# One conformer block on one core: the first FFN's SiLU products turned by the DMA crossbar instead of TensorE, and its adaLN rows read on another schedule

## The chip, the cores and the metric

The kernel runs on one core of a Trainium2 chip. The metric is the device time of one execution in microseconds (us). Before the change three executions gave a median of 1824.64 us (1823.7 to 1827.11).

## What is computed

One block of a macaron network on 256 tokens of width 2048, in float32: FFN, mixer (differential attention beside a causal depthwise convolution), FFN. Nine modulation vectors come from one product of `silu(c)` with `w_ada` (adaLN), three for each part: shift, scale and gate.

```python
ada = silu(c) @ w_ada + b_ada
sh1, sc1, g1, shm, scm, gm, sh2, sc2, g2 = split(ada, 9)
h = modulate(rms_norm(x, ffn1_norm), sh1, sc1)
x = x + 0.5 * g1 * swiglu(h, ffn1_w_gu, ffn1_w_down)     # D_FF = 5632
h = modulate(rms_norm(x, mix_norm), shm, scm)
x = x + gm * hybrid_mixer(h, ...)
h = modulate(rms_norm(x, ffn2_norm), sh2, sc2)
x = x + 0.5 * g2 * swiglu(h, ffn2_w_gu, ffn2_w_down)

def swiglu(h, w_gu, w_down):
    g, u = split(h @ w_gu, 2)
    return (silu(g) * u) @ w_down
```

## The kernel before, in words

**Weight tiles.** Every weight matrix is read in tiles of 1 MB, `raw` (128 partitions x 4 x 512 float32), by DMAs that SyncE issues in order (SP's queue, line 295; four `raw` buffers). To multiply float32 in the faster fp32r format, each half of a tile is split in two: ScalarE rounds it to `whi` (line 306), VectorE subtracts to get the rest, `wlo` (line 308); there are four `whi` and four `wlo` buffers of half a tile. TensorE then makes three products for each of the 4 x 2 pairs of a 128-row slice and a token half (lines 330, 334, 335), 24 matmuls of 512 columns a tile.

**The first half of an FFN.** The 5632 columns of gate and up are cut into 22 chunks of 256 + 256 columns, each with four weight tiles (2048 rows in fours of 512). The first pass of the rows for all chunks comes first (`stage_a`, while the norm and the modulation are still being made), then in the first FFN some later rows of the chunks 3 to 14 (the lists `EARLY`). What is left is done chunk by chunk in the loop over `groups`: chunks 0 to 2 together, then each alone. In the first FFN chunks 3 to 12 have two tiles left there, 13 and 14 one, 15 to 21 three. In the second FFN chunks 3 to 5 have two left, all later ones three.

**`finish(c)`**, the code under change, runs one weight tile after a chunk's last product. VectorE adds the partial sums out of PSUM (line 854, once for each token half), ScalarE takes SiLU (line 855), VectorE multiplies by up (line 856). The down product needs the result with the columns on the partitions, so it must be turned. That is `rest()`, put off by one more weight tile (`after_tiles(1, rest)`). In the first FFN TensorE turns it, with four 128 x 128 transposes into PSUM (line 875). In the second FFN the DMA crossbar does: ScalarE first copies the float32 words into two planes of 16-bit halves (line 860, `planes`), a DMA transpose on SP's queue turns both (line 866, `turned`), and ScalarE puts the halves together again (line 869, `src`). Either way the turned product is then split like a weight, ScalarE at line 351 and VectorE at line 352.

**The adaLN rows.** `w_ada` is read in 144 rows of 1 MB into the same four `raw` buffers by the same queue (line 193); VectorE multiplies each by `silu(c)` and sums it (line 194). Where the rows stand in the program is set by two schedules. During the first part of the first FFN `DUE` gives, for so many 512-row quarters of weight tiles done, how many rows must have been asked for, with straight lines between its points. In the loop over single chunks and in the down product, `ada_share(r, limit)` asks for `r` rows a weight tile until row `limit`.

**What sets the order.** The instructions of each engine and of SP's queue are put in an order when the program is built, by a scheduler that goes by the order of the code and an estimate of when inputs are ready. On the chip each engine runs its list in that order: what waits holds up all behind it.

Of the kernel before, what the change touches and what calls it, by code (L numbers as in the profile page):

```python
# [31 lines left out]
NCH = 22  # L32
# [13 lines left out]
AGAIN = [4, 5, 6]  # L46
EARLY = [[3, 8, 9], [4, 5, 6], [7, 10, 11], [12, 13, 14]]
EARLY_3 = [13, 14]

DUE = ((8, 4), (16, 6), (22, 8), (57, 16), (108, 24), (151, 32))  # L50


TAPS = (6, 5, 6, 6, 6, 6, 8, 6, 6, 6)
# [3 lines left out]

SEVEN = (3, 5, 8, 10, 13, 15, 17)
KEPT = 6
CROSSBAR = {0: False, 96: True}  # L60
RMS_EPS = 1e-6
LN_EPS = 1e-5
LAM_INIT = 0.8 - 0.6 * float(np.exp(-0.3 * 0))
# [20 lines left out]
def block_kernel(ctx: ExitStack, tc: tile.TileContext, x_in, pos_in, w_ada, small, w_gu1, w_dn1,  # L84
# [20 lines left out]
    def blk(shape, dtype=F32):  # L105
        return blkp.tile(shape, dtype, tag="blk", name=nm("blk"))

    def tmp(shape, dtype=F32):
        return tmpp.tile(shape, dtype, tag="tmp", name=nm("tmp"))

    def sm(shape, tag="sm"):
        return smp.tile(shape, F32, tag=tag, name=nm(tag))
# [4 lines left out]
    def tp_tile(shape=(P, 512)):  # L117
        return tpp.tile(list(shape), F32, tag="tp", name=nm("tp"))
# [53 lines left out]
    def after_tiles(n, fn):  # L172
        later.append([n, fn])
# [34 lines left out]
    def ada_due(rows):  # L208

        r0, j0 = DUE[0]  # L210
        for r, j in DUE[1:]:
            if rows <= r:
# [137 lines left out]
    def split_from_psum(tp, hi, lo):  # L350
        nc.scalar.copy(out=hi, in_=tp)  # L351
        nc.vector.tensor_sub(out=lo, in0=tp, in1=hi.bitcast(F32))  # L352
# [310 lines left out]
    def ffn(st, w_gu, w_dn, gate_base, ada_a, ada_b, nxt, again, early, early_3):  # L663
# [6 lines left out]
        base = st.base  # L670
# [180 lines left out]
        def finish(c, accs):  # L851
            p = parts[c]
            for t in range(NT):
                nc.vector.tensor_add(out=p[:, t, :], in0=accs[t], in1=p[:, t, :])  # L854
                nc.scalar.activation(out=p[:, t, :256], in_=p[:, t, :256], func=AF.Silu)  # L855
                nc.vector.tensor_mul(out=p[:, t, 256:], in0=p[:, t, :256], in1=p[:, t, 256:])  # L856

            if CROSSBAR[base]:
                planes = tmp([P, 2, NT, 256], U16)
                nc.scalar.copy(out=planes, in_=p[:, :, 256:].bitcast(U16).rearrange("p t (f b) -> p b t f", b=2))  # L860

            def rest():
                a = blk([P, 2, 2, S], F32R)
                if CROSSBAR[base]:
                    turned = tmp([P, 2, NT, 2, P], U16)
                    nc.sync.dma_start_transpose(out=turned.rearrange("p b t i s -> p (b t i) s"),
                                                in_=planes.rearrange("p b t f -> p (b t f)"))
                    src = tmp([P, 2, NT, P])
                    nc.scalar.copy(out=src.bitcast(U16).rearrange("p i t (s b) -> p b t i s", b=2), in_=turned)  # L869
                    src = src.rearrange("p i t s -> p i (t s)")  # L870
                else:
                    src = tp_tile((P, 2, S))
                    for t in range(NT):
                        for i in range(2):
                            nc.tensor.transpose(src[:, i, t * P:(t + 1) * P],  # L875
                                                p[:, t, 256 + i * P:256 + (i + 1) * P], ident)
                split_from_psum(src, a[:, 0], a[:, 1])
                aT[c] = a

            after_tiles(1, rest)  # L880
# [3 lines left out]
        for g in groups:  # L884
            accs = {c: [acc_tile() for _ in range(NT)] for c in g}
            for i, (pc, ks) in enumerate(segments(g[0], start_of[g[0]], 4)):
                ada_until(base + 8 * pc + 8)
                pieces(last_part[0])
                for c in g:
                    w = w_tile(w_gu[c, pc], False, ks)  # L890
                    mm_tile(accs[c], w, act, 4 * pc, i == 0, pc == 3, (0, 1), ks)
                    ext[c] = 4
                    if len(g) > 1:
                        ada_a_share(ks[1] - ks[0])
                        pieces(last_part[0])
                    else:
                        ada_share(ada_b[0], ada_b[1])
                    if i == 0:
                        while pend:
                            finish(*pend.pop(0))  # L900
            for c in g:
                pend.append((c, accs[c]))
# [24 lines left out]
        if nxt is None:  # L927
            down_strassen(w_dn, aT, a_act, lambda: gate(gate_base, 0.5), evac_last, lambda: ada_share(*ada_b),
                          pend, finish)
            return  # L930

        prev = None
        for n in range(4):
            accs = [acc_tile() for _ in range(NT)]
            held = []
            for pc in range(11):
                hold = n == 3 and pc >= 11 - HOLD_DN
                w = w_tile(w_dn[n, pc], hold and pc > 11 - HOLD_DN)
                ada_share(ada_b[0], ada_b[1])
                if hold:  # L940
                    held.append((pc, w))
                    continue
                mm_tile(accs, w, a_act, 4 * pc, pc == 0, pc == 10)
                if pc == 0:
                    while pend:
                        finish(*pend.pop(0))
                    if prev is not None:
                        evac(*prev)
                        prev = None
                if n == 0 and pc == 6 and nxt is norm_m:  # L950
                    attention_constants()
                if n == 0 and pc == 2:
                    gbc = gate(gate_base, 0.5)
# [74 lines left out]
    norm1 = Norm(0, "n1", sm([P, NT, 4], "ss"))  # L1028
    norm_m = Norm(48, "nm", sm([P, NT, 4], "ss"), DVE_COLS)
    norm2 = Norm(96, "n2", sm([P, NT, 4], "ss"))  # L1030


    ffn(norm1, w_gu1, w_dn1, 32, (0.78, 32), (0.78, 104), norm_m, AGAIN, EARLY, EARLY_3)


    st = norm_m
# [462 lines left out]
```

## Time and profile before

| | |
|---|---|
| median of three executions | 1824.64 us |
| the profiled execution | 1823.93 us, of which the profile's span is 1822.2 us |
| TensorE (PE) busy | 1797.5 us, 99% |
| VectorE (DVE), ScalarE (ACT) busy | 1518.2 us (83%), 1023.9 us (56%) |
| read from HBM | 492.37 MB, 271 GB/s over the span |
| line 875, the first FFN's transposes | 88, between 284.0 and 528.4 us |
| line 866, the second FFN's DMA transposes | 22, between 1293.8 and 1589.6 us |

The profile is that of one execution. A row of its timeline gives start, duration, engine (SPq is SP's queue of DMA issues), line, operation and "output<-inputs" by the program's names; rows of one kind that follow each other are merged with a count. In square brackets stands the idle time before the row and what ended it. A row of the groups of lines gives busy time, mean duration in ns, and idle time ahead of it with its releasers. A row of the windows gives, for a stretch of the span, the busy time of each engine with the number of instructions, the granted TensorE clock (1.00 is full), the share in which the 16 DMA engines moved something, and what they moved in GB/s.

### The profile page before, as it was taken

How to read it: one execution, taken by the hardware profiler on the slowest of the kernel's cores; microseconds unless marked ns; L12 is line 12 of the kernel's file. 1: busy time of each engine (PE TensorE's matmuls, PEld its weight loads, DVE VectorE, ACT ScalarE, POOL GpSimd, SP SyncE). 2: the span in 40 equal slices, each digit the busy share in tenths (PEclk: the TensorE clock that was granted, in tenths of full speed). 3: DMA queues.
4: the chain of work that ended last, by engine and by line, in shares of the span. 5: the costliest groups of instructions: out<-in, count | busy, mean ns of one | idle time of the engine just before them, and what ended most of it. 6: DMA issues, size and time to landing. Idle time of an engine off the chain costs nothing.

```text
span 1822.2 us, 21874 instructions
## 1 busy us (share of the span) xinstructions
PE 1797.5 (99%) x8093; PEld 1481.0 (81%) x8093; DVE 1518.2 (83%) x2018; ACT 1023.9 (56%) x1533; POOL 28.3 (2%) x29
## 2 busy tenths in 40 slices
PE   7999999999999999999999999999999999999998
PEld 5788888888888887888888888888888888878887
DVE  7889869999888787898999798777788765599877
ACT  7554444444444343566798657675666566555453
POOL 0000000000000000000110100000000000000000
PEclk8999999999999999999999999999999999999999
DMA  9977978888889988775444487889888976655552
GB/s 378 359 304 299 351 271 300 328 322 338 338 326 352 353 342 333 292 265 208 166 158 160 152 343 255 329 326 318 265 304 303 303 244 213 206 204 216 200 217 107
DMA packets 102298, 503.26 MB, mean 276 GB/s; under 512 B 37760, under 2 KB 38192, under 8 KB 44720
## 3 DMA queue, kind: packets, MB, share of 16 engines
q1 hardware_dynamic: 102192, 501.87, 75.1%
q8 instruction: 63, 1.03, 0.2%
q14 instruction: 43, 0.35, 0.0%
HBM read 492.37 MB, written 2.12 MB: 271 GB/s over the span
## 4 chain that ended last, share of the span: by engine, by line
PE 86%; DVE 7%; ACT 3%; DMA 2%; issue 2%; POOL 0%; SPq 0%; POOLq 0%; DVEq 0%; ACTq 0%
PE acc L334 27%; PE acc L335 27%; PE acc L330 27%; DVE wlo L308 2%; DMA tmp<-tmp 1%; PE tp L334 1%; PE tp L335 1%; PE tp L330 1%; ACT whi L306 1%; DVE raw L194 1%; DMA blk<-in_w_gu_dram 1%; PE acc L1161 1%; DVE wlo L537 1%; DVE blk L1053 1%; PE tp L875 1%
## 5 line engine op out<-in xcount | busy, mean ns | idle before, releaser
L334 PE MATMUL acc<-wlo,blk 128*128 128x512 f32 x2340 | 912.7, 390 | 6.7 <-DVE wlo L308 6.6
L330 PE MATMUL acc<-whi,blk 128*128 128x512 f32 x2343 | 912.8, 392 | 1.8 <-ACT blk L404 1.3
L335 PE MATMUL acc<-whi,blk 128*128 128x512 f32 x2340 | 912.2, 390 | 0.1
L306 ACT CAST whi<-raw 128x1024 fp32r<-128x1024 f32 (+1 forms) x581 | 599.6, 1044 | 497.1 <-PE acc L335 362.8
L308 DVE TENSOR_TENSOR wlo<-raw,whi 128x1024 fp32r<-128x1024 f32 (+1 forms) x581 | 692.8, 1210 | 179.2 <-ACT whi L306 177.7
L334 PEld LDWEIGHTS acc<-wlo,blk 128*128 128x128 f32 x2340 | 439.5, 188 | 101.2 <-DVE wlo L308 11.3
L330 PEld LDWEIGHTS acc<-whi,blk 128*128 128x128 f32 x2343 | 440.0, 188 | 93.3 <-ACT blk L404 1.7
L335 PEld LDWEIGHTS acc<-whi,blk 128*128 128x128 f32 x2340 | 439.3, 188 | 92.3 <-DVE blk L406 0.7
L194 DVE CUSTOM_DVE_ANT_0 raw<-raw,c_bc 128x2048 f32<-128x2048 f32 x142 | 324.3, 2285 | 14.2 <-DMA raw<-in_w_ada_dram 14.0
L536 ACT CAST whi<-raw 128x1024 fp32r<-128x1024 f32 (+1 forms) x56 | 53.0, 946 | 67.9 <-PE tp L335 33.6
L537 DVE TENSOR_TENSOR wlo<-raw,whi 128x1024 fp32r<-128x1024 f32 (+1 forms) x56 | 60.8, 1087 | 18.9 <-ACT whi L536 18.6
L1053 DVE SCALAR_TENSOR_TENSOR blk<-blk,cst,blk 128x245 f32<-128x245 f32 (+21 forms) x176 | 70.4, 455 | 0.5 <-ACT blk L1051 0.5
L690 ACT COPY blk<-acc 128x512 f32<-128x512 f32 x72 | 41.6, 588 | 42.7 <-PE acc L335 40.1
L854 DVE TENSOR_TENSOR blk<-acc,blk 128x512 f32<-128x512 f32 x88 | 56.8, 683 | 0.2
L869 ACT COPY tmp<-tmp 128x1024 uint16<-128x1024 uint16 x22 | 29.8, 1355 | 47.4 <-DMA tmp<-tmp 47.4
L855 ACT ACTIVATE blk<-blk 128x256 f32<-128x256 f32 x88 | 34.2, 414 | 23.4 <-DVE blk L854 23.3
L330 PE MATMUL acc<-blk,blk 128*128 128x512 f32 x104 | 40.7, 395 | 0.7 <-ACT blk L322 0.7
L334 PE MATMUL acc<-blk,blk 128*128 128x512 f32 x100 | 39.1, 391 | 0.0
L335 PE MATMUL acc<-blk,blk 128*128 128x512 f32 x100 | 38.9, 393 | 0.0
L352 DVE TENSOR_TENSOR blk<-tmp,blk 128x512 fp32r<-128x512 f32 x22 | 15.1, 688 | 26.3 <-ACT blk L351 26.3
L856 DVE TENSOR_TENSOR blk<-blk 128x256 f32<-128x256 f32 x88 | 34.0, 418 | 0.2 <-ACT blk L855 0.2
L860 ACT COPY tmp<-blk 128x1024 uint16<-128x1024 uint16 x22 | 22.9, 1042 | 11.8 <-DVE blk L856 11.6
(231 smaller groups left out, 1064.2 us busy)
## 6 DMA issues: line engine op xcount, KB each, us to landing
raw<-in_w_gu_dram SPq DMA_DIRECT2D x161, 1024.0 KB, 5.9
raw<-in_w_ada_dram SPq DMA_DIRECT2D x142, 1024.0 KB, 6.3
raw<-in_w_dn_dram SPq DMA_DIRECT2D x88, 1024.0 KB, 5.1
raw<-in_w_in_dram SPq DMA_DIRECT2D x40, 1024.0 KB, 4.8
raw<-in_w_out_dram SPq DMA_DIRECT2D x16, 1024.0 KB, 5.0
raw<-in_w_gu_dram SPq DMA_DIRECT2D x8, 768.0 KB, 6.1
blk<-in_w_gu_dram SPq DMA_DIRECT2D x10, 512.0 KB, 13.8
blk<-gate_line SPq DMA_DIRECT2D x6, 512.0 KB, 5.0
```

What stands on the lines that cost most here:

```text
L194: nc.vector.tensor_tensor_reduce(out=raw, in0=raw, in1=c_bc, scale=1.0, scalar=0.0, op0=ALU.mult, op1=ALU.add, accum_out=ada_cols[g][:, j ...
L306: nc.scalar.copy(out=hi[:, :m, :], in_=rw)
L308: nc.vector.tensor_sub(out=lo[:, :m, :], in0=rw, in1=hi[:, :m, :].bitcast(F32))
L330: nc.tensor.matmul(acc, ah, wh, start=start, stop=False)
L334: nc.tensor.matmul(acc, ah, wl, start=False, stop=False)
L335: return nc.tensor.matmul(acc, al, wh, start=False, stop=stop)
L536: nc.scalar.copy(out=hi[:, :n, :], in_=src)
L537: nc.vector.tensor_sub(out=lo[:, :n, :], in0=src, in1=hi[:, :n, :].bitcast(F32))
L690: last_part[0] = nc.scalar.copy(out=parts[c][:, t, :], in_=accs[t])
L854: nc.vector.tensor_add(out=p[:, t, :], in0=accs[t], in1=p[:, t, :])
L855: nc.scalar.activation(out=p[:, t, :256], in_=p[:, t, :256], func=AF.Silu)
L1053: nc.vector.scalar_tensor_tensor(out=y[:, d:], in0=u, scalar=w, in1=y[:, d:], op0=ALU.mult, op1=ALU.add)
```

## The change

Three constants and a test. `CROSSBAR` becomes, for each FFN, the chunks whose products the crossbar turns: all 22 in both. `DUE` gets one more point, so that six more adaLN rows (32 to 37) are asked for by quarter 180 of the first part. In the first FFN's chunk loop and down product 0.7 rows come with a weight tile, not 0.78.

```diff
-DUE = ((8, 4), (16, 6), (22, 8), (57, 16), (108, 24), (151, 32))
+DUE = ((8, 4), (16, 6), (22, 8), (57, 16), (108, 24), (151, 32), (180, 38))
-CROSSBAR = {0: False, 96: True}
+CROSSBAR = {0: range(NCH), 96: range(NCH)}
...
-            if CROSSBAR[base]:
+            if c in CROSSBAR[base]:
                 planes = tmp([P, 2, NT, 256], U16)
...
             def rest():
                 a = blk([P, 2, 2, S], F32R)
-                if CROSSBAR[base]:
+                if c in CROSSBAR[base]:
                     turned = tmp([P, 2, NT, 2, P], U16)
...
-    ffn(norm1, w_gu1, w_dn1, 32, (0.78, 32), (0.78, 104), norm_m, AGAIN, EARLY, EARLY_3)
+    ffn(norm1, w_gu1, w_dn1, 32, (0.78, 32), (0.7, 104), norm_m, AGAIN, EARLY, EARLY_3)
```

VectorE's list where one of the two-tile chunks of the first FFN is finished (its partial sums and product lie in the buffer blk_254; the next chunk's are in blk_276), before:

```order
L352 TENSOR_TENSOR blk_2477<-tp_2478,blk_2477 128x512
L856 TENSOR_TENSOR blk_254<-blk_254 128x256 x2
L198 TENSOR_TENSOR ada_2306<-ada_2306,cst 128x2
L194 ISA raw_2616,ada_2306<-raw_2616,c_bc 128x2048
L194 ISA ada_2306 128x1
L308 TENSOR_TENSOR wlo_2586<-raw_2582,whi_2584 128x1024
L308 TENSOR_TENSOR wlo_2590<-raw_2582,whi_2588 128x1024
L308 TENSOR_TENSOR wlo_2629<-raw_2625,whi_2627 128x1024
```

And now:

```order
L856 TENSOR_TENSOR blk_254<-blk_254 128x256 x2
L308 TENSOR_TENSOR wlo_2564<-raw_2560,whi_2562 128x1024
L308 TENSOR_TENSOR wlo_2568<-raw_2560,whi_2566 128x1024
L194 ISA raw_2601,ada_2459<-raw_2601,c_bc 128x2048
L194 ISA ada_2459 128x1
L308 TENSOR_TENSOR wlo_2610<-raw_2606,whi_2608 128x1024
L854 TENSOR_TENSOR blk_276<-acc_2516,blk_276 128x512
L308 TENSOR_TENSOR wlo_2614<-raw_2606,whi_2612 128x1024
L352 TENSOR_TENSOR blk_2594<-tmp_2597,blk_2594 128x512
L194 ISA raw_2640,ada_2459<-raw_2640,c_bc 128x2048
L194 ISA ada_2459 128x1
L856 TENSOR_TENSOR blk_276<-blk_276 128x256
```

In both lists line 352 of a chunk stands ahead of line 856 of the next chunk. Before, its input came from TensorE's transposes (tp_2478); now it comes (tmp_2597) by way of line 860, the DMA and line 869, and four halves of weight tiles stand between line 856 and it. ScalarE's list changes with it: after the SiLU of blk_254 come two halves of a weight tile, the copy of line 860, one half, the copy of line 869, which reads what the DMA transpose wrote, one half, and line 351; all that stands behind line 869 waits for the DMA with it.

SP's queue at the same chunk; a load of w_ada is an adaLN row. Before, loads only:

```order
L193 DMA raw_2525<-in_w_ada_dram 128x2048
L295 DMA raw_2534<-in_w_gu_dram 128x2048
L193 DMA raw_2576<-in_w_ada_dram 128x2048
L295 DMA raw_2582<-in_w_gu_dram 128x2048
L193 DMA raw_2616<-in_w_ada_dram 128x2048
L295 DMA raw_2625<-in_w_gu_dram 128x2048
```

And now:

```order
L866 DMA_TRANSPOSE tmp_2506<-tmp_2469 128x8x128
L295 DMA raw_2560<-in_w_gu_dram 128x2048
L193 DMA raw_2601<-in_w_ada_dram 128x2048
L295 DMA raw_2606<-in_w_gu_dram 128x2048
L866 DMA_TRANSPOSE tmp_2595<-tmp_2558 128x8x128
L193 DMA raw_2640<-in_w_ada_dram 128x2048
L295 DMA raw_2652<-in_w_gu_dram 128x2048
```

Between two loads there is now a DMA transpose, which waits for the planes of line 860 (tmp_2558), and the loads behind it wait with it.

SP's queue ahead of the chunk loop, where the six rows go (the tiles of w_gu are the last that the lists EARLY ask for and the first of chunks 0 to 2). Before:

```order
L295 DMA raw_1928<-in_w_gu_dram 128x2048
L295 DMA raw_1990<-in_w_gu_dram 128x2048
L295 DMA raw_2024<-in_w_gu_dram 128x2048
L295 DMA raw_2058<-in_w_gu_dram 128x2048
L295 DMA raw_2092<-in_w_gu_dram 128x2048
L295 DMA raw_2126<-in_w_gu_dram 128x2048
L295 DMA raw_2160<-in_w_gu_dram 128x2048
L295 DMA raw_2196<-in_w_gu_dram 128x2048
```

And now:

```order
L295 DMA raw_1928<-in_w_gu_dram 128x2048
L193 DMA raw_1991<-in_w_ada_dram 128x2048
L295 DMA raw_1994<-in_w_gu_dram 128x2048
L295 DMA raw_2028<-in_w_gu_dram 128x2048
L193 DMA raw_2062<-in_w_ada_dram 128x2048
L295 DMA raw_2066<-in_w_gu_dram 128x2048
L193 DMA raw_2100<-in_w_ada_dram 128x2048
L295 DMA raw_2103<-in_w_gu_dram 128x2048
L193 DMA raw_2137<-in_w_ada_dram 128x2048
L295 DMA raw_2141<-in_w_gu_dram 128x2048
L193 DMA raw_2175<-in_w_ada_dram 128x2048
L295 DMA raw_2178<-in_w_gu_dram 128x2048
```

Where weight tiles followed each other without a row between them, a row now stands behind nearly every tile.

## The prediction

> **What bounds the kernel now.** I read the page first, then the windows, then TensorE's timeline.
>
> ```profile
> span 1822.2 us, 21874 instructions
> PE 1797.5 (99%) x8093; PEld 1481.0 (81%) x8093; DVE 1518.2 (83%) x2018; ACT 1023.9 (56%) x1533; POOL 28.3 (2%) x29
> PE 86%; DVE 7%; ACT 3%; DMA 2%; issue 2%; POOL 0%; SPq 0%; POOLq 0%; DVEq 0%; ACTq 0%
> ```
>
> TensorE is busy 99% of the span and is 86% of the chain that ended last. So an instruction taken from it shortens the kernel by its issue time, as long as weights keep coming. The windows show how near the others are to their limits (columns: stretch, length, busy PE, PEld, DVE, ACT, POOL, clock, DMA share, GB/s): the stretch ahead of the chunk loop, the two-tile chunks, the down product, and the second FFN's chunk loop, which has the crossbar already.
>
> ```profile
> 227.80:273.30 45.50, 45.50 (x202) 37.68 (x201) 30.65 (x35) 20.70 (x25) 0.00 (x0) 1.00 0.73 271
> ...
> 364.40:409.90 45.50, 45.50 (x212) 37.62 (x211) 44.26 (x58) 22.61 (x31) 0.00 (x0) 1.00 0.85 322
> ...
> 592.10:637.70 45.60, 45.60 (x203) 37.77 (x202) 35.38 (x36) 17.83 (x17) 0.00 (x0) 1.00 0.92 353
> ...
> 1366.50:1412.00 45.50, 45.50 (x202) 37.66 (x202) 36.96 (x44) 27.76 (x32) 0.00 (x0) 1.00 0.87 303
> ```
>
> VectorE is at 44.26 of 45.50 in the two-tile chunks (rows overlap their neighbours a little, so it has somewhat more room than that), and the DMA engines at 0.85.
>
> **What is removed.** Line 875's four transposes in each of 22 chunks:
>
> ```profile
> L875 PE MATMUL tp<-cst,blk x88: 270/272/327, 284.0 to 528.4; 128*128 128x128 f32 x88
> ...
> 395.90 0.39 PE L330 MATMUL acc<-whi,blk 128*128 128x512 f32 x1
> ...
> 398.39 0.40 PE L335 MATMUL acc<-whi,blk 128*128 128x512 f32 x1
> 398.63 0.60 PE L875 MATMUL tp<-cst,blk 128*128 128x128 f32 x4
> 398.98 0.48 PE L330 MATMUL acc<-whi,blk 128*128 128x512 f32 x1
> 399.30 0.40 PE L334 MATMUL acc<-wlo,blk 128*128 128x512 f32 x1
> 399.54 0.39 PE L335 MATMUL acc<-whi,blk 128*128 128x512 f32 x1
> ```
>
> Matmuls are pipelined, so starts count, not durations: 11 steps from 395.90 to 398.39 are 0.2264 each. From 398.39 to 399.54 lie three such steps, 0.68, and 1.15 passes: a group of four costs 0.47. All lie on the path: 22 x 0.47 = **10.3 us gained**. A weight tile is 24 steps, 5.44 us, and a chunk with two tiles left 10.88, where it took 11.35.
>
> **What is added.** Rows of the second FFN price it:
>
> ```profile
> L869 ACT COPY tmp<-tmp 128x1024 uint16<-128x1024 uint16 x22 | 29.8, 1355 | 47.4 <-DMA tmp<-tmp 47.4
> L860 ACT COPY tmp<-blk 128x1024 uint16<-128x1024 uint16 x22 | 22.9, 1042 | 11.8 <-DVE blk L856 11.6
> L351 ACT CAST blk<-tmp 128x512 fp32r<-128x512 f32 x22 | 13.6, 618 | 0.3
> L351 ACT CAST blk<-tp 128x512 fp32r<-128x512 f32 x22 | 12.7, 580 | 1.4 <-PE tp L875 1.4
> L352 DVE TENSOR_TENSOR blk<-tmp,blk 128x512 fp32r<-128x512 f32 x22 | 15.1, 688 | 26.3 <-ACT blk L351 26.3
> ...
> DMA to landing us min/median/max: 3.4/4.5/8.3
> ```
>
> ScalarE: 22 x (1.355 + 1.042 + 0.04) = 54 us. It was busy about half of 364 to 410, so as work this fits (5.4 + 2.4 of 10.88 a chunk); line 352 costs VectorE what it did. Rows at 0.7 and not 0.78 take 0.16 rows, about 0.4 us, from VectorE in a two-tile chunk. As work, nothing exceeds TensorE's 10.88. The price is the waiting. In its list VectorE does line 352 of a chunk ahead of line 856 of the next, so the turn is a link of a chain from chunk to chunk: 856, 860, transpose, 869, 351, 352, and so to the next 856. A turn in the second FFN at its usual speed:
>
> ```profile
> 1378.18 0.75 DVE L856 TENSOR_TENSOR blk<-blk 128x256 f32<-128x256 f32 x2
> ...
> 1386.46 0.69 DVE L352 TENSOR_TENSOR blk<-tmp,blk 128x512 fp32r<-128x512 f32 x1 [2.99 <-ACT blk L351]
> ...
> 1378.96 1.05 ACT L860 COPY tmp<-blk 128x1024 uint16<-128x1024 uint16 x1 [2.33 <-DVE blk L856]
> ...
> 1384.41 1.36 ACT L869 COPY tmp<-tmp 128x1024 uint16<-128x1024 uint16 x1 [2.50 <-DMA tmp<-tmp]
> ```
>
> From the end of 856 (1378.93) to the end of 352 (1387.15) 8.2 us pass, in which both engines stood still for 2.5 to 3.0. To this comes what stands between 352 and the next 856: from nothing up to a row (2.29), partial sums and a half tile, some 2 us on average by the new list. So a link takes 8.2 + 2 = 10.2 and just fits into 10.88. Where tiles are dense the turn is slower, and the second FFN has one such place, its chunks 3 to 5 with two tiles left:
>
> ```profile
> 1298.03 1.05 ACT L306 CAST whi<-raw 128x1024 fp32r<-128x1024 f32 x1 [1.66 <-PE acc L335]
> ...
> 1337.10 1.37 ACT L869 COPY tmp<-tmp 128x1024 uint16<-128x1024 uint16 x1 [4.53 <-DMA tmp<-tmp]
> ...
> 1306.22 0.42 DVE L856 TENSOR_TENSOR blk<-blk 128x256 f32<-128x256 f32 x1
> ...
> 1328.84 0.75 DVE L856 TENSOR_TENSOR blk<-blk 128x256 f32<-128x256 f32 x2
> ...
> 1340.55 0.68 DVE L352 TENSOR_TENSOR blk<-tmp,blk 128x512 fp32r<-128x512 f32 x1
> ...
> 1345.89 0.76 DVE L856 TENSOR_TENSOR blk<-blk 128x256 f32<-128x256 f32 x2
> ...
> PE acc L334 <- DVE wlo L308: 0.9, 1, 0.9
> ```
>
> These rows are of ScalarE, then VectorE, then TensorE's waits from 1270 to 1400. At 1298 ScalarE still waited for TensorE to free a buffer: the weights were as far ahead as four buffers allow. At 1337 it had waited 4.53 us for a transpose, the turn from 1329.59 to 1341.23 took 11.6, and TensorE itself waited 0.9. The lead had gone. From chunk 3's line 856 (ends 1306.64) to chunk 6's (1346.65) 40.0 us pass for seven tiles, 7 x 5.44 = 38.1: 0.6 too much in each of three chunks, with 0.5 rows a tile.
>
> **The sum for the first FFN.** Its chunks 3 to 12 are ten of these in a row, with 0.7 rows a tile. The 0.4 rows more in a chunk are 0.9 us of VectorE; about half stand behind 352 in the new list, so on the chain: 0.6 + 0.5 = 1.1 too much a chunk, 11 us. The bounds are none (10.2 fits) and 11.6 + 2 - 10.88 = 2.7 a chunk, 27 us; I take the row of the like place, nearer the lower end. The three turns of chunks 0 to 2 come together: the second FFN's lost its lead in them and the next three chunks; that lead is at most two of four half-tile buffers ready, 2 x 2.72 = 5.4 (estimate), so 5.4 + 0.9 - 1.9 = 4.4 went there. I take the same. Chunks 13 and 14 have one tile each, shorter than any link, but the new list puts 856 of 14 ahead of 352 of 13: 1 us each (bounds 0 and 4), 2. In chunks 15 to 21 a link has 16.3 us and costs nothing. The lead pays 5.4. Stalls: 11 + 4.4 + 2 - 5.4 = **12.0**. Net 12.0 - 10.3 = +1.7 on the profiled execution's 1823.93, which is 0.7 below the median; on the median, **1826 us**.
>
> The six rows ahead of the loop: 6 x 2.29 = 13.7 us of VectorE on its 30.65 in the first quoted window, 44.4 of 45.5. The loads, 1.83 of 1.049 MB in 5.44 us, are 353 GB/s, which the third window shows held. The rows are hidden there, at the price of a smaller lead at chunk 0 (0 to 3 us, kept for the range). Fewer rows in the down product free 0.2 us of VectorE a tile where nothing waits: no gain.
>
> **The rivals.** *The cover holds.* Most turns go at 8.2, the chain fits, only slow transposes and chunks 13 and 14 cost: stalls of 0 to 6, 1814.3 to 1820.3, likeliest 1817. For it: the median landing is 4.5, that of the usual turn, and TensorE waited 0.9 us once in 130 us with the crossbar. Against: that place ran three dense chunks, not ten, and used the whole lead.
>
> *The DMA engines fill up, every turn is a slow one, and it is slower.*
>
> ```profile
> 1364.03 1.24 SPq L866 DMA_TRANSPOSE tmp<-tmp  x1
> ...
> 1396.09 1.24 SPq L866 DMA_TRANSPOSE tmp<-tmp  x1
> ```
>
> 353 GB/s at 0.92 is 384 at full share. The window from 1366 to 1412, with the three transposes from 1364 to 1396, moved 303 x 45.5 = 13.8 MB, 35.9 us at that rate, in 0.87 x 45.5 = 39.6: a transpose takes 1.2 us of all engines. A two-tile chunk then needs 3.4 x 1.049 MB / 384 + 1.2 = 10.5 of 10.88, a share of 0.97, with four raw buffers and a queue that stops at each transpose until its planes are made. A transpose issued into full queues lands late, and the turn takes the 11.6 of the dense place: 2.7 too much a chunk. With all ten slow it is 27 + 4.4 + 4 - 5.4 = 30, with half of them 16.5: 1831 to 1844, likeliest 1836. It decides from a mean turn of about 10.2; the forecast's is 10.0, the cover's at most 8.9, where a link passes 10.88. For it: 0.85 without transposes now. Against: 0.92 was held for 45 us.
> The Trainium skill (Advanced Engine Details and Errata, X-Bar Transpose) says that such transposes run about as fast as other DMAs, 350 to 400 GB/s; by that a turn's 128 x 8 x 128 words of 16 bits, 0.26 MB, would take 0.7, a chunk 10.0 (estimates), and this rival would be rarer. The 1.2 us speaks against it.
>
> *The crossbar holds up all loads while it turns.* If the 4.5 us to landing were all taken from the loads, a chunk would need 9.3 + 4.5 = 13.8, ten of them 29 more, 24 beyond the lead, and the time 1838 or more. Against: in the window above this would have left 45.5 - 13.5 = 32 us for 13.8 MB, 430 GB/s. The Trainium skill (VectorE: DVE Perf Modes, The three transpose paths) puts a 128 x 128 turn at 1309 ns by the crossbar and 390 by TensorE, and advises TensorE where the result may lie in PSUM; the trace agrees in the order (4.5 us for eight 16-bit blocks, 0.47 of TensorE), not in the price of one. That the change doesn't turn all 22 is ruled out by SP's new list, which has 22 transposes more.
>
> **How the numbers follow.** A measurement tells about 0.2%, 3.7 us, from no change. Forecast: 0.46, stalls of 8 to 17, 1822 to 1831, of it 0.28 within 0.2% and 0.18 slower. Cover holds: 0.32, faster. Slow turns: 0.19, and held-up loads: 0.03, both slower. So faster 0.32, same 0.28, slower 0.40. The range runs from 1815, leaving out the last of the cover's case, to 1836, leaving out the worse half of the slow turns and the held-up loads.
>
> **What would show it.** Line 875 gone, TensorE's 512-column step unchanged. Right: TensorE waits for wlo of some 12 us between 290 and 410, VectorE's line 352 waiting for 351, ScalarE's 869 for the DMA with 2 to 5 us a chunk, lines 856 about 12 us apart. The cover's case: no waits of TensorE, 856 every 10.9. Slow turns: 856 over 13 apart, line 869 waiting over 4, a DMA share over 0.93. A changed clock, or stalls outside 240 to 530, would make it wrong.

## The result and the profile after

The changed kernel took 1836.67 us (median of four, 1835.37 to 1837.83), the kernel before on the same chip 1825.73 (1823.7 to 1827.11): a ratio of 1.0063, 95% interval [1.0052, 1.0075]. It is slower by 0.6%, and 0.7 us above the end of the range; 1826 was forecast. The profiled execution took 1835.75 us.

Of the profile's page, span, busy times and the chain by engine and by line:

```profile
span 1834.0 us, 21728 instructions
PE 1795.1 (98%) x8005; PEld 1470.0 (80%) x8005; DVE 1520.1 (83%) x2018; ACT 1070.4 (58%) x1577; POOL 29.2 (2%) x29
PE 73%; DVE 13%; DMA 6%; ACT 4%; issue 3%; SPq 0%; POOL 0%; POOLq 0%; DVEq 0%; ACTq 0%
PE acc L334 23%; PE acc L335 23%; PE acc L330 23%; DVE wlo L308 5%; DMA raw<-in_w_gu_dram 3%; DVE raw L194 2%; ACT whi L306 2%; DMA tmp<-tmp 1%; PE tp L334 1%; PE tp L335 1%; DMA raw<-in_w_ada_dram 1%; PE tp L330 1%; DMA raw<-in_w_dn_dram 1%; PE acc L1161 1%; DVE wlo L537 1%
```

TensorE has its 88 transposes fewer (8093 to 8005 instructions), and still the span is 11.8 us longer. Its share of the chain falls from 86% to 73%; VectorE and the DMA take most of the difference. Loads of w_gu into `raw` are new among the chain's largest parts, with 3%; the DMA transposes (tmp<-tmp) have 1%, as before. Between 240 and 560 us, the stretch of the change, the loads of w_gu are 16.7% of the chain and the transposes 3.2%. The three stretches of the first FFN that the prediction showed, by the same columns:

```profile
227.80:273.30 45.50, 43.93 (x192) 35.72 (x192) 36.61 (x40) 17.32 (x21) 0.00 (x0) 1.00 0.86 331
364.40:409.90 45.50, 43.40 (x188) 34.66 (x187) 40.68 (x51) 29.73 (x37) 0.00 (x0) 1.00 0.91 306
592.10:637.70 45.60, 45.60 (x202) 37.75 (x202) 35.63 (x37) 19.22 (x20) 0.00 (x0) 1.00 0.89 339
```

In the chunk loop (the second row) VectorE has gone from 44.26 down to 40.68, and the DMA engines move less, 306 and not 322 GB/s, though their share is up from 0.85 to 0.91: nobody works at a limit, yet TensorE stands for 2.1 us. So something waits. The waits between 240 and 560 us, first of the engines, then of SP's queue (waiter, line, what it waited for: us in total, times, longest):

```profile
ACT whi L306 <- DMA raw<-in_w_gu_dram: 40.8, 25, 3.2
ACT blk L855 <- DVE blk L854: 40.0, 17, 4.4
DVE wlo L308 <- ACT whi L306: 28.1, 31, 3.1
...
ACT tmp L869 <- DMA tmp<-tmp: 23.1, 16, 3.1
PE acc L334 <- DVE wlo L308: 13.8, 22, 1.5
...
DVE blk L352 <- ACT blk L351: 2.9, 3, 1.1
```

```profile
SPq L866 <- ACT whi L306: 65.8, 11, 9.2
SPq L866 <- ACT tmp L860: 58.4, 9, 7.9
...
SPq L866 <- ACT blk L855: 6.3, 1, 6.3
...
SPq L866 <- ACT blk L351: 3.4, 1, 3.4
```

And the two largest waits of SP's queue in the kernel before, in the same stretch:

```profile
SPq L193 <- DVE wlo L308: 69.0, 23, 5.0
SPq L295 <- DVE ada L194: 68.3, 24, 4.5
```

Before, SP's queue waited almost only for a buffer to come free (VectorE done with `wlo` or with a row), so a load went out as soon as it could. Now it stands for 134 us (65.8 + 58.4 + 6.3 + 3.4) at transposes whose planes ScalarE has not made yet. All loads behind them stand too, and ScalarE waits 40.8 us, in 25 places, for tiles of w_gu; before, it waited for none there. Rounding waits, so `wlo` waits, so TensorE waits. The forecast's own link, VectorE's line 352 waiting for the turned product, is 2.9 us in all. ScalarE also waits 40.0 us at the SiLU for VectorE's partial sums; this is no loss by itself, for in a run below that is 11 us faster (still planes) the same wait is 70.1 us.

One period of it, late in the loop, with three tiles a chunk: SP's queue, then ScalarE, then VectorE.

```profile
431.67 1.23 SPq L866 DMA_TRANSPOSE tmp<-tmp  x1
433.00 0.53 SPq L295 DMA_DIRECT2D raw<-in_w_gu_dram  x1
433.63 0.38 SPq L193 DMA_DIRECT2D raw<-in_w_ada_dram  x1
435.01 2.54 SPq L295 DMA_DIRECT2D raw<-in_w_gu_dram  x2
441.90 0.33 SPq L193 DMA_DIRECT2D raw<-in_w_ada_dram  x1
448.77 1.23 SPq L866 DMA_TRANSPOSE tmp<-tmp  x1
450.10 0.53 SPq L295 DMA_DIRECT2D raw<-in_w_gu_dram  x1
```

```profile
434.74 1.36 ACT L869 COPY tmp<-tmp 128x1024 uint16<-128x1024 uint16 x1 [1.19 <-DMA tmp<-tmp]
...
438.42 2.00 ACT L306 CAST whi<-raw 128x1024 fp32r<-128x1024 f32 x2 [1.67 <-DMA raw<-in_w_gu_dram]
...
447.70 1.05 ACT L860 COPY tmp<-blk 128x1024 uint16<-128x1024 uint16 x1 [0.38 <-DVE blk L856]
```

```profile
439.50 2.36 DVE L308 TENSOR_TENSOR wlo<-raw,whi 128x1024 fp32r<-128x1024 f32 x2 [1.70 <-ACT whi L306]
441.78 2.29 DVE L194 CUSTOM_DVE_ANT_0 raw<-raw,c_bc 128x2048 f32<-128x2048 f32 x1
443.99 0.08 DVE L194 DVE_READ_ACCUMULATOR2_ANT ada<- 128x1 f32 x1
```

VectorE is done with a row at 444.07, and its `raw` buffer is free. But at the head of the queue is the transpose of 448.77, which waits for line 860 (447.70 to 448.75). The next load goes right behind it, at 450.10, 6.0 us after the buffer came free. One period earlier the load that went at 433.00, also right behind a transpose, is the one that ScalarE waits for until 438.42. The loop closes: the late load makes `wlo` late, this makes the sums, the SiLU and the planes late, and these the next transpose. The chain that ended last takes this very way here, from the load of 433.00 by lines 306, 308, 194, 854 to 856 and 860 to the transpose at the head of the queue.

### The profile page after: what moved, and what is told of

The parts are those of the page before. It is cut to its first block, busy times and chain, and to the rows that moved or that the text cites. A ratio compares the mean times of both kernels' runs of the same rounds, so it can differ in the third digit from the quotient of the medians.

```text
span 1834.0 us, 21728 instructions
## 1 busy us (share of the span) xinstructions
PE 1795.1 (98%) x8005; PEld 1470.0 (80%) x8005; DVE 1520.1 (83%) x2018; ACT 1070.4 (58%) x1577; POOL 29.2 (2%) x29
## 4 chain that ended last, share of the span: by engine, by line
PE 73%; DVE 13%; DMA 6%; ACT 4%; issue 3%; SPq 0%; POOL 0%; POOLq 0%; DVEq 0%; ACTq 0%
PE acc L334 23%; PE acc L335 23%; PE acc L330 23%; DVE wlo L308 5%; DMA raw<-in_w_gu_dram 3%; DVE raw L194 2%; ACT whi L306 2%; DMA tmp<-tmp 1%; PE tp L334 1%; PE tp L335 1%; DMA raw<-in_w_ada_dram 1%; PE tp L330 1%; DMA raw<-in_w_dn_dram 1%; PE acc L1161 1%; DVE wlo L537 1%
## 5 line engine op out<-in xcount | busy, mean ns | idle before, releaser
L869 ACT COPY tmp<-tmp 128x1024 uint16<-128x1024 uint16 x44 | 59.8, 1359 | 67.0 <-DMA tmp<-tmp 66.8
L1053 DVE SCALAR_TENSOR_TENSOR blk<-blk,cst,blk 128x247 f32<-128x247 f32 (+21 forms) x176 | 70.5, 458 | 0.0
L855 ACT ACTIVATE blk<-blk 128x256 f32<-128x256 f32 x88 | 34.6, 413 | 56.9 <-DVE blk L854 56.7
L860 ACT COPY tmp<-blk 128x1024 uint16<-128x1024 uint16 x44 | 45.8, 1043 | 20.9 <-DVE blk L856 20.5
L352 DVE TENSOR_TENSOR blk<-tmp,blk 128x512 fp32r<-128x512 f32 x44 | 30.2, 687 | 26.0 <-ACT blk L351 25.9
```

The lines of the kernel that those rows point to most:

```text
L1053: nc.vector.scalar_tensor_tensor(out=y[:, d:], in0=u, scalar=w, in1=y[:, d:], op0=ALU.mult, op1=ALU.add)
```

## The experiments

Four explanations were put to the chip. **Queue**: the loads stand in SP's queue behind a transpose that waits for its planes. **DMA**: the transposes take the DMA engines' time from the loads. **Chain**: the prediction's, a turn delays VectorE's line 352 and with it the next chunk. **Rows**: the six rows moved ahead of the loop and the new places of the others. Each run's time is a median; the kernel before ran beside it. Runs that add a line ahead of the code shift the line numbers by one (`wlo` is then 309), the later turn the transpose to 868 and the join to 875.

To place the losses I use one quantity, worked out from the start times of the matmuls: the time from one start to the next less 0.2267 us for each 512-column step, summed over a stretch (differences of less than some 0.03 us left out). It holds TensorE's stalls and its transposes. The table, like every trace, is of one profiled execution; the one of "later, 0.78 rows" took 1831.52 us, 3.0 more than the median of its run.

```
stretch (us)          200-290 290-400 400-430 430-540 540-760 760-1100  whole run
before                    1.4     4.4     1.3     2.8     2.1     37.6       76.4
after                     3.8     7.0     4.2     6.7     0.9     38.1       87.6
rows only                 3.8     4.0     1.5     2.9     0.5     37.7       77.3
turned later              3.8     4.7     2.0     1.7     0.7     37.4       77.7
still planes              3.8     4.0     2.4     2.1     0.7     37.5       77.6
late chunks only          1.5     4.4     0.9     3.8     5.6     38.2       80.9
later, 0.78 rows          0.0     5.4     3.3     3.6     6.4     39.1       84.0
later, 0.55 rows          0.0     5.4     0.0     0.0     4.1     49.3       89.7
later, 0.62 rows          0.0     0.8     0.0     0.1     7.4     43.9       80.8
eight chunks later        1.5     2.3     1.3     2.8     5.9     37.6       77.7
```

Before's 9.9 between 200 and 540 are the transposes themselves, so it had no stall there; after's 21.7 there are stalls alone, against a forecast of 12.0. The difference of the two, 11.8, is what the span grew by.

**The two halves of the change.** Rows alone:

```diff
-CROSSBAR = {0: range(NCH), 96: range(NCH)}
+CROSSBAR = {0: (), 96: range(NCH)}
```

> The new schedule of the adaLN rows alone: TensorE turns the first FFN's products as before. Four theories. Queue (the loads stand in SP's queue behind a transpose that waits for its planes), DMA (the engines are full) and chain (the turn delays VectorE's next chunk, as predicted): as before, 1823 to 1828 us, for without transposes none of them has a cause. Rows (six rows ahead of the chunk loop and their place in VectorE's list make the loss): 1830 to 1837, with TensorE waiting for wlo between 260 and 280 us.

1825.81 us against 1823.82, 1.0011 [1.0002, 1.002], as Queue, DMA and Chain expected. Rows falls as the main cause. It is the whole of one small loss, though, ahead of the loop; VectorE in this run:

```profile
261.86 0.69 DVE L854 TENSOR_TENSOR blk<-acc,blk 128x512 f32<-128x512 f32 x1 [4.35 <-PE acc L335]
262.46 2.35 DVE L308 TENSOR_TENSOR wlo<-raw,whi 128x1024 fp32r<-128x1024 f32 x2
```

VectorE stands 4.35 us at a partial sum whose product isn't done, with two halves of `wlo` behind it; TensorE then stands three times between 262 and 277 us, 3.2 us here and 3.8 in the changed kernel, where VectorE waits 5.48 us at 261.38 in the same order. The kernel before has no stall there.

The crossbar alone:

```diff
-DUE = (..., (108, 24), (151, 32), (180, 38))
+DUE = (..., (108, 24), (151, 32))
-    ffn(norm1, w_gu1, w_dn1, 32, (0.78, 32), (0.7, 104), ...)
+    ffn(norm1, w_gu1, w_dn1, 32, (0.78, 32), (0.78, 104), ...)
```

> The crossbar for all 22 chunks of the first FFN with the old schedule of rows (no point at 180, 0.78 a tile). Queue: the loss stays, 1832 to 1838. DMA: more than the change, 1838 to 1842, since 0.78 and not 0.7 rows of 1 MB come with a tile in the chunk loop. Chain: 1836 to 1840, a little more work of VectorE on each link. Rows: the gain of 10 us shows, 1814 to 1818.

1839.55, 1.0088 [1.0074, 1.0102]: in the ranges of DMA and Chain, 1.6 us above Queue's. So the crossbar is the slow half, and with the old rows it is slower than with the new ones. This run alone does not tell why.

**Another queue for the transposes.** Line 866 is issued from ScalarE's queue in the first FFN:

```diff
-nc.sync.dma_start_transpose(
+(nc.sync if base else nc.scalar).dma_start_transpose(
```

> The changed kernel with the first FFN's 22 transposes issued from ScalarE's DMA queue, so that SP's loads never stand behind one; data, DMA engines and the turn's steps stay. Queue: the waits of TensorE after 290 us go nearly all, 1818 to 1824. DMA: the same bytes on the same engines, 1834 to 1838. Chain: the same turn, a little longer by the issue on ScalarE, 1836 to 1840. Rows: 1834 to 1838.

1902.58, 1.0437 [1.0416, 1.0457]: every theory missed. It frees SP's queue as meant, and makes a worse wait. The transposes' landing times, and the waits between 240 and 560:

```profile
DMA to landing us min/median/max: 4.2/6.7/15.1
```

```profile
ACT tmp L869 <- DMA tmp<-tmp: 87.7, 20, 11.8
DVE wlo L308 <- ACT whi L306: 41.5, 17, 8.7
DVE blk L352 <- ACT blk L351: 36.6, 10, 12.6
```

Now ScalarE waits for tiles of w_gu only 10.0 us, and the transpose lands behind the loads, in 6.7 us (15.1 at most) where it took 3.1 in the changed kernel. ScalarE stands at line 869, and behind it stand the halves that it should round. Here the turn really is a link that holds up line 352 (36.6 us, 2.9 in the changed kernel). The run doesn't tell Queue from the others, since it put a new cost in place of the old. The same with the rows of before:

> As the run before, with the old schedule of rows too. Queue: 1814 to 1820, the 10 us of the transposes with few waits. DMA: 1837 or more. Chain: 1836 to 1840. Rows: 1814 to 1818.

1933.62, 1.0605 [1.059, 1.062], the same miss, larger; only DMA's range, which had no upper end, holds it. The Trainium skill (DMA: Bandwidth & Descriptors, Queues, rings and completion order) says that SP and ScalarE each have a queue on the same 16 engines and that a transfer's completion is a write that lands only after every earlier write of its engine, across queues. The trace of the first of these two runs agrees: a transpose landed 1.3 us (median) behind the last load that SP's queue had issued before it or within 0.2 us after it.

**The join later.** The transpose stays where it is in SP's queue; line 869, and what follows from it, is put off by one weight tile more (`rest` is cut in two, `turn` and `join`). In ScalarE's list two or three halves of a tile now stand between planes and join, where one to three stood:

```diff
+TURN, JOIN = 1, 2
...
-            after_tiles(1, rest)
+                after_tiles(TURN, turn)
+                after_tiles(JOIN, join)
```

> The changed kernel with line 869 and what follows put off by one weight tile more; the transposes stay where they are in SP's queue. In ScalarE's list one half tile more stands between the planes and line 869. Queue (the loads behind a transpose come late because the queue waits for its planes; that ScalarE's own queue made it worse is put down to transposes that land late among loads): 1834 to 1839, as the changed kernel. Chain (the length of the turn as VectorE meets it): 1824 to 1831. DMA (the engines are full): 1834 to 1839.

1836.74, 1.007 [1.0055, 1.0085]: in the ranges of Queue and DMA, outside Chain's. ScalarE's wait at the join for the transposes has fallen from 23.1 to 14.4 us and the time is that of the changed kernel, so shortening this wait brought nothing. The link itself was hardly loosened, though: line 352 (353 here) still stands ahead of line 856 of the next chunk for most chunks and waits 5.3 us in all. What speaks against Chain is therefore the changed kernel's trace more than this run: its line 352 waits 2.9 us where TensorE loses 21.7, and in the chain that ended last a transpose's landing stands only three times between 240 and 560 us (at 399, 407 and 517). No run here cuts the link and leaves the queue standing. SP's queue stands as in the changed kernel:

```profile
SPq L867 <- ACT whi L307: 71.7, 11, 9.0
SPq L867 <- ACT tmp L861: 64.1, 9, 9.1
...
SPq L867 <- ACT tmp L874: 11.6, 2, 6.4
```

**The transpose later in the queue.** The same cut, with the transpose itself behind the loads of about a chunk later, when its planes have long been made:

```diff
+TURN, JOIN = 3, 4
...
+                with tc.issue_after(w_dma[0].ins) if base == 0 else nullcontext():
                     nc.sync.dma_start_transpose(...)
```

> Both the transpose, in SP's queue, and line 869 stand about a chunk later, so that the planes are long made when the queue comes to the transpose. Queue: SP waits little at line 866, the loads come in time, 1817 to 1827. Chain: 1817 to 1827 too. DMA: the same bytes, 1834 to 1839.

1825.72, 1.0009 [1.0, 1.0018]: 11 us back. DMA falls here; Queue and Chain expected the same time, for line 353 of a chunk now stands behind line 857 of the next. The waits of SP's queue at the transposes, between 240 and 560:

```profile
SPq L868 <- ACT whi L307: 11.1, 4, 3.9
SPq L868 <- ACT blk L352: 9.6, 2, 6.3
SPq L868 <- ACT tmp L875: 5.0, 2, 4.5
SPq L868 <- ACT tmp L861: 3.3, 1, 3.3
SPq L868 <- DVE wlo L309: 2.7, 1, 2.7
SPq L868 <- PE acc L336: 2.4, 1, 2.4
SPq L868 <- DMA tmp<-tmp: 0.5, 1, 0.5
```

134 us have become 34.6. The turns themselves take about 20 us each now (chunk 15's line 857, which was 856, ends at 424.05, its line 353 at 446.33: 22.3), where the changed kernel's took 8 to 9; a turn two and a half times as long costs nothing, once nothing that is due stands behind it.

**The same queue, with nothing to wait for.** The transpose stays in its place and of its size, but reads a part of x that has lain in SBUF since the start, and line 869 copies the planes. This leaves out that the first FFN's products are turned.

```diff
-in_=planes.rearrange("p b t f -> p (b t f)"))
+in_=planes.rearrange(...) if base else xall[:, 0, :512].bitcast(U16))
...
-in_=turned)
+in_=turned if base else planes.rearrange("p b t (i s) -> p b t i s", i=2))
```

> The changed kernel with one edit: in the first FFN the crossbar transposes a part of x that has lain in SBUF since the start, at the same place in SP's queue and of the same size, and line 869 copies the planes themselves, so that nothing waits for the transposed tile. It leaves out that the products are turned, so the first FFN's output is another one; every instruction and byte stays. Queue theory: SP no longer stands at the transpose, the loads behind it are on time: 1818 to 1828 us. DMA theory: the transposes move as many bytes and the loads stay late: 1833 us or more. Chain theory: line 869 no longer waits for the crossbar, so VectorE's line 351 is early: 1820 to 1828 us too, but then SP's waits do not matter, and this run cannot tell it from Queue; the run with line 869 a tile later already did.

1824.89, 1.0002 [0.9993, 1.001]. As many transposes, bytes and instructions, and 11 us less: DMA falls as the main cause. The queue's waits at them, then the landing times:

```profile
SPq L866 <- PE acc L335: 1.0, 1, 1.0
SPq L866 <- DMA tmp<-xall: 0.6, 1, 0.6
```

```profile
DMA to landing us min/median/max: 5.8/6.9/9.8
```

The transposes land in 6.9 us, not 3.1, behind loads that have just gone out, and it does no harm. Since line 869 waits for no transpose here, Chain would have this run fast too; what speaks against Chain is the 2.9 us that line 352 waits in the changed kernel.

**Fewer bytes.** In the changed kernel, adaLN rows 38 to 69 are loaded to a quarter, and VectorE multiplies `silu(c)` by itself in their place; the modulation by these rows is left out.

```diff
+        few = 38 <= j < 70
+        nc.sync.dma_start(out=raw[:, :512] if few else raw, in_=...)
```

> The changed kernel with the adaLN rows 38 to 69, those read during the chunk loop, loaded to a quarter, and VectorE's product of them made of other data of the same size (it leaves these rows' modulation out). In the chunk loop the DMA engines have a third less to move; each engine's list stays. DMA: the waits go, 1818 to 1826. Queue: the loads still stand behind the transposes, 1831 to 1837. Chain: 1831 to 1837.

1829.75, 1.0035 [1.002, 1.0049]: 5 to 7 of the 11 us go (by the ratios, by the times), and the time lies between the ranges. A load that is late by the queue hurts less when the ones beside it are short, so this run does not decide between Queue and DMA.

**Chunks 15 to 21 alone**, with the rows of before, by `CROSSBAR = {0: range(15, NCH), ...}`:

> The kernel before, with its schedule of rows, and the crossbar only for chunks 15 to 21 of the first FFN, which have three tiles each. Queue: each chunk loses what TensorE gains, as in the changed kernel, where such a chunk took 16.9 us and not 16.8: 1824 to 1828. DMA and chain: a chunk has 16.3 us for a turn of 8 to 9 and 15.7 of transfers, the 7 x 0.47 us are gained: 1820 to 1823.

1828.49, 1.0023 [1.0014, 1.0032], in no range, 0.5 us above Queue's. The prediction held that these seven cost nothing, which would have brought 3.3 us; the kernel loses 4. The stalls begin only at 498 us: by the table 3.8 up to 540, where the transposes had taken 2.8, and 5.6 behind, in the down product, where the kernel before had 2.1.

**Where the gain went.** Turned later, or with still planes, the kernel only gets back to the time of before, though the transposes' 10 us are gone from TensorE. By the table 12.2 us of stalls are left between 200 and 540 with the later turn. Four more runs tried to keep the gain, and a fifth asked whether bytes are the limit. With the rows of before:

> The later turn with the rows of before (old list of due rows, 0.78 a tile). Tells what the row half of the change is worth once the queue is free. Queue theory: 1821 to 1827 us, since the stalls at 200 to 290 us fall from 3.8 to 1.5 us and the loop loads one row in nine more. Rows theory (the six rows are what eats the gain): 1816 to 1821 us. DMA theory (engines full in the chunk loop, 0.78 rows worse than 0.7): above 1830 us.

1828.54, 1.0021 [1.0012, 1.003], in none of the ranges. The stalls at 200 to 290 are gone, and those from 400 on grow. With fewer rows in the loop:

```diff
-    ffn(norm1, w_gu1, w_dn1, 32, (0.78, 32), (0.7, 104), ...)
+    ffn(norm1, w_gu1, w_dn1, 32, (0.78, 32), ((0.55, 0.85), 104), ...)
```

> The transpose and line 869 stand about a chunk later, as in the run that did this alone; besides, the list of due rows is that of before (six rows fewer ahead of the loop) and the chunk loop takes 0.55 rows a weight tile instead of 0.7, the down product 0.85. Queue theory: with SP's queue free and fewer row loads in the loop, the loads of weights are on time; the stall of some 2.4 us at 262 to 277 us goes with the six rows, and the TensorE time saved by the 22 chunks' transposes (10 us) is kept: 1814 to 1821 us, faster than the kernel before. DMA theory: the rows are only moved to the down product and the transposes still take their 1.2 us of all engines each: at or above 1826 us. Chain theory: the order of VectorE's list is nearly that of the run with the later turn: 1824 to 1828 us.

1836.64, 1.0057 [1.0045, 1.0069], a miss of 15 us for Queue; DMA's range, with no upper end, holds it, but the loss is not where DMA has it. The chunk loop got what was meant (nothing lost from 400 to 540), but some eight rows were still to be asked for before the mixer's second half, and they came in one burst. SP's queue there, and ScalarE behind it:

```profile
1043.40 17.60 SPq L194 DMA_DIRECT2D raw<-in_w_ada_dram  x6
1062.96 0.33 SPq L296 DMA_DIRECT2D raw<-in_w_out_dram  x1
```

```profile
1070.43 1.99 ACT L307 CAST whi<-raw 128x1024 fp32r<-128x1024 f32 x2 [17.68 <-DMA raw<-in_w_out_dram]
```

Six row loads, each of which must wait for VectorE to free a buffer, hold up a load of w_out until 1062.96, and TensorE stands 9.4 us. It is the same fault as that of the transposes: one queue, in order, with a due load behind something that has to wait. With 0.62 rows in the loop and 0.87 in the down product:

> The later turn with the old list of due rows, 0.62 rows a weight tile in the chunk loop and 0.87 in the down product. Against the run with 0.55 and 0.85 this takes some five rows out of the burst of row loads at 1043 to 1061 us, behind which a load of the next weights came 9.4 us late there. Queue theory: the burst shrinks to about four rows, the stall at 1062 us is gone, and what stalls are left in the chunk loop lie between that run's 6.6 us and the 12.0 us of the later turn with the changed rows: 1820 to 1824 us. DMA theory (the engines are full in the loop, and any row more there costs): 1824 to 1830 us.

1828.22, 1.0021 [1.0012, 1.0031], another miss for Queue; it lies in DMA's range, but not for DMA's reason. From 200 to 540 only 0.9 us is left of before's 9.9, so the loop keeps the whole gain. It is given back behind: 7.4 against 2.1 from 540 to 760, 43.9 against 37.6 from 760 to 1100. ScalarE's waits for the down product's tiles, 540 to 760 us, before and here:

```profile
ACT whi L306 <- DMA raw<-in_w_dn_dram: 27.8, 11, 4.0
```

```profile
ACT whi L307 <- DMA raw<-in_w_dn_dram: 69.9, 23, 5.3
```

The rows that the loop no longer asks for stand among the loads of the down product. To see whether bytes were the limit in the loop, the later turn with the quarter rows (which leaves out the same modulation):

> The later turn with the changed rows; of adaLN rows 38 to 69 only a quarter is loaded, and VectorE multiplies c_bc by itself in their place, so that every instruction and its order stay and 25 MB of loads go. It leaves out the modulation that these rows give. Engines full (what is left after the queue): the 8 us of stalls in the chunk loop go, those at 262 to 277 us stay: 1815 to 1820 us. Order of VectorE's and ScalarE's work: the stalls stay, 1823 to 1828 us. In the earlier run with these quarter rows and the transposes in their old place the time was 1829.75 us; it should be beaten by 8 us or more in the first case.

1826.36, 1.0007 [0.9998, 1.0016]. The stalls of the loop stay, though the DMA share from 400 to 540 falls to 0.78 (1.01 with the rows whole). So bytes aren't what keeps the later turn from gaining; the expectation of full engines falls. One stall is the largest in either run, 3.4 us in the step from 304.8 (2.7 at 305.5 with the rows whole). There the joined turns of chunks 0 to 2 stand together in the lists: ScalarE does lines 875 and 352 (869 and 351 in the changed kernel), twice over, ahead of the rounding that TensorE waits for:

```profile
300.35 2.55 ACT L875 COPY tmp<-tmp 128x1024 uint16<-128x1024 uint16 x2
302.77 1.13 ACT L352 CAST blk<-tmp 128x512 fp32r<-128x512 f32 x2
303.81 0.41 ACT L856 ACTIVATE blk<-blk 128x256 f32<-128x256 f32 x1
304.12 1.03 ACT L307 CAST whi<-raw 128x1024 fp32r<-128x1024 f32 x1
```

These rows are of the later turn with the rows whole. Last, the later turn for chunks 3 to 10 alone, with the rows of before:

> The rows of before (old list, 0.78 a tile); the crossbar turns chunks 3 to 10 alone, later in SP's queue, and TensorE turns the other fourteen as before. Gain on TensorE 8 times 0.47 us, 3.8 us. Engines full: eight transposes at 1.2 us of all engines each are 9.6 us of DMA in a stretch of 90 us that had 14 in 100 free before, 12.6 us: the loads stay on time and the time is 1820 to 1823 us. If each transposed chunk cost what it did in the run with 22 chunks and the old rows (12 us of stalls against 10 of gain at 290 to 540): 1825 to 1827 us.

1824.64, 1.0 [0.9991, 1.0008], between the two ranges. The loop saves 2.1 us of 8.5 (290 to 540), and 540 to 760 takes 3.8 more. No version here beats the kernel before. Why the stretch from 540 to 760 takes 4 to 7 us in every run of the table that joins the crossbar with the old list of due rows, where the changed list leaves less than 1, and which order of the lists would keep both, stays open.

## Why the prediction was wrong, point by point

- *A group of four transposes costs 0.47 us of TensorE, 10.3 in all.* Right: TensorE has 88 instructions fewer, its 512-column step is unchanged, and before's 9.9 us between 200 and 540 are gone.
- *"The price is the waiting", in a chain through line 352.* This is the step that failed. The turn from 856 to 352 was shorter than forecast, 8.6 us on average in chunks 3 to 12 (10.0), the transpose landed in 3.1 (4.5), line 869 waited 1.05 us a chunk for it (2 to 5), and line 352 waited 2.9 us in all. Yet from chunk 3's line 856 (ends 293.33) to chunk 12's (398.16) a chunk takes 11.65 us, close to the forecast's 12. The spacing came out for a wrong reason, by luck: VectorE hardly waited in the link.
- *What took its place* is SP's queue, which stands 134 us at the transposes; without that standing (still planes, later turn) 11 us come back. The prediction had "a queue that stops at each transpose until its planes are made", as a remark in a rival on DMA shares, and gave it no price of its own. It could have been read from the lists: a chunk has one transpose in SP's queue, line 860 comes late in it, and all loads behind it stand, up to 9.2 us.
- *"In chunks 15 to 21 a link has 16.3 us and costs nothing."* Wrong in the changed kernel, and the largest term missed: 6.7 us of stalls from 430 to 540. For a link, three tiles a chunk are room; for a queue they are not, since each chunk's transpose still stands between loads. Where these chunks alone were changed, the stalls began only at 498 us; that the loads were late already when chunk 15 came may be part of it, and was not tested.
- *Chunks 3 to 12: 11, less a lead of 5.4*, with *4.4* for the bundle and *2* for chunks 13 and 14: 12.0. From 290 to 430 measured 7.0 + 4.2 = 11.2. As a size it is near, mostly by another mechanism. Only from chunk 12 to 14 (13 and 14 have one tile) does the chain that ended last run as forecast, from line 856 (398.16) by 860, the transpose, 869 and 352 to the next 856 (406.21); the stalls at 404 and 411 us are 2.4, where 2 were forecast for it.
- *The six rows are hidden ahead of the loop (0 to 3 us).* Their work is hidden, their place in VectorE's list is not: 3.8 us of stalls at 262 to 277, where before had none. The run with the rows alone has 3.2 there and is 2 us slower on the median.
- *The sum.* 11.2 + 6.7 + 3.8 = 21.7 of stalls, where 12.0 were forecast: the miss of some 10 us is the chunks 15 to 21, put at nothing, and the rows, left to the range.
- *The rivals.* The transposes' 1.2 us of all engines (still planes: 1824.89 with all of them) and the crossbar holding up loads while it turns are not the cause either. The slow turns' 1836 is met by luck: their sign was a mean turn over 10.2 and lines 856 over 13 apart, and the runs show 8.6 and 11.65. The Trainium skill's advice (VectorE: DVE Perf Modes, Rules for kernel authors) to let TensorE transpose where the result may lie in PSUM is borne out by every version tried here: none with the crossbar in the first FFN is faster than the kernel before.

## What to carry to other kernels

A DMA that waits for a result of the engines doesn't belong in the queue that feeds these engines, unless the result is ready when its turn comes: look at what stands behind it, and ask how long after its buffer came free each load goes out. Cost a new instruction in each queue that it joins before costing the chain of its own result. And when freed engine time doesn't shorten a stretch, or only moves its stalls, look at the schedule of the loads behind it before trying a third setting.

## What the runs showed of the hardware that was not expected

- A transpose lands fast when the queue is in trouble. In the changed kernel it took 3.1 us (median), as the last load ahead of it landed 1.4 us (median) after the transpose went out. With the queue flowing that load landed 5.6 (turned later) and 5.9 us (still planes) after, the transpose 1.0 behind it, 6.7 and 6.9 in all, and the kernel was 11 us faster.
- Issued from ScalarE's queue, away from the loads, the same transposes took 6.7 us at the median and up to 15.1.
- In the run with ScalarE's queue the granted clock was 0.90 from 300 to 430 us, where TensorE stood 9.3 us at a time (from 294 on) and 5.4 (at 356), and 0.984 over the span; the changed kernel, whose stalls there are 1.6 us at most, kept 1.00. TensorE was busy 1817.2 us for the same 8005 instructions, against 1795.1, so the run's 1902.58 is not stalls alone.
